# The order of a layer's small TensorE products: runs of full-height tiles, then of half-height tiles, partition halves alternating

## The chip, the cores and the metric

The kernel runs on one core of one Trainium2 chip. The metric is device time in microseconds (us), the median of several runs. A profile shows one further execution.

## What is computed

Two layers of a hybrid sequence model on 528 tokens (16 learned meta tokens ahead of 512) of width 1024. In each layer one wide projection feeds four mixers. Three of them work in chunks of tokens and matter here. The reference, cut down:

```python
def hybrid_layer(x, ...):
    h = rmsnorm(x, norm_mix) * mask
    (hg_q, hg_f, hg_i, hg_g, rt_q, rt_k, rt_v, rt_g, ss_u,
     gd_qkv, gd_b, gd_a, gd_g, gate) = _split(h @ w_in, IN_SPLITS)
    branches = (hgrn2_branch(...), retention_branch(...), s5_branch(...), gdn_branch(...))
    merged = sum over m of sigmoid(gates[m]) * (branches[m] @ w_branch[m])
    x = x + merged @ w_out
    h2 = rmsnorm(x, norm_ffn)
    gt, up = jnp.split(h2 @ w_gu, 2, axis=-1)
    return x + (jax.nn.silu(gt) * up) @ w_down

# gated linear attention and retention, chunk by chunk, 4 heads of 64 key and 128 value features
att = masked(q_t @ k_t.T)                # inside a chunk
o   = att @ v + q_t @ S                  # S: state handed over from the chunks before
S   = decay * S + k_end.T @ v
# gated delta rule: a unit triangular system per chunk and head
uw = triangular_solve(a0 + eye, rhs, lower=True, unit_diagonal=True)
```

## The kernel before

All weights are float32 and are split into a high and a low part of twelve bits; each panel of 128 columns is multiplied as high by high, high by low and low by high. These big products (`mmk`, line 206) are the main stream of TensorE: an operand tile of 128 by 128 against 264 or 256 tokens at a time. The mixers' own products are small and in plain float32. They are written as Python generators (`ret_gen` for retention, `gla_gen` for gated linear attention, `gdn_gen` for the gated delta rule, `s5_*` for the state space branch). A main-stream product calls `pump` before every fourth step of its contraction, and `pump` lets each running generator go on to its next `yield`. So TensorE's instruction order is exactly the order in which the program is written; a scheduler orders the other engines. What a generator emits between two yields is called a section below. A chunk has 128 tokens; there are four, and a short first one of 16.

A small product uses only the part of the 128 by 128 array that its operand covers. A profile row writes that as rows*columns. A state of one head has 64 rows, and two heads share the 128 partitions: head pair `p` = 0 lies on partitions 0 to 63 and `p` = 1 on 64 to 127.

- Outputs of a chunk in retention (lines 537 and 540) and in gated linear attention (lines 746 and 749): for each of the four heads, first `att @ v` with a 128*128 operand, then `q @ S` with a 64*128 operand added onto it. In the text the first kind is F (full height), the second H (half height). The order is F H F H F H F H.
- Blocks inside a chunk in gated linear attention: for `p` = 0 the products of blocks of 64 tokens (line 713, 64*64), then those between blocks of 16 (`cross`, line 695, 64*16); then the same for `p` = 1. Two later calls of `cross` do blocks of 32 and 64 in the same way.
- The triangular inverse in the gated delta rule, blocks of 32*32: two sections for a first product (line 1103, row blocks 0 and 2, 16 products each), then two for the next (lines 1112 and 1113 for row blocks 1 and 0, then 1113 for 2). `next(run)` (the first chunk's own work, lines 1040 and 1059 first) stands at the end of the second and the fourth section.

Every result goes to a PSUM tile of the pool `px` (`psx`), which has four buffers, and is read from there by ScalarE or VectorE: `tn_a` squares (line 371) and scales (line 382) the heads, `copy_predicated` (line 718) masks the blocks. In the last layer the short chunk has no outputs (`mute`).

Of the kernel before, what the change touches and what calls it, by code (L numbers as in the profile page):

```python
# [64 lines left out]
class Kern:  # L65
    """The main stream (projections, merges, feed forward) is plain code; the mixers between the projections are
    generators, whose parts are laid between its products: `pump` lets each running one go on to its next yield."""
# [112 lines left out]
    def wload(self, src, kt):  # L180
        """src [128, kt * 128]; returns k -> (high part, low part)"""
# [35 lines left out]
    def mm2(self, ws, kt, xh, xl, segs):  # L217
        """two products, both without their last operands at first: those come while others are used"""
# [46 lines left out]
    def rowpow(self, dst, src, scale, n):  # L265
        """dst = (src * scale + EPS) ** -0.5, tokens on partitions"""
# [51 lines left out]
    def norm_h(self, g):  # L318
        """finish of a norm: the operands hh, hl of the products that follow"""
# [15 lines left out]
    def norm_finish(self, h, n=KD):  # L335
        """the next n parts of a half"""
# [6 lines left out]
    def tail_hooks(self, kt):  # L343
        """the norm's first half, while the second half of its last operands is computed"""
# [3 lines left out]
    def head(self, srcs, segs):  # L348
        """the first two products after a norm, with its second half between those of the first"""
# [4 lines left out]
    def silu2(self, dst, ps, segs):  # L354
        """dst = 2 silu(ps)"""
# [31 lines left out]
    def tn_b(self, dst, c0, n, on, order):  # L387
        """dst[:, :, c0:c0+n] gets the normalised heads with features on partitions"""
# [6 lines left out]
    def head_gates(self, l, ct, segs):  # L395
        """2 silu of the gate columns of the heads"""
# [6 lines left out]
    def head_finish(self, gen, o, gs, ng, segs):  # L403
        """normalised heads times weight and gates; parts in float32r"""
# [44 lines left out]
    def mute(self, l, ci):  # L449
        """whether a chunk has only keys and values: the last layer's outputs for the meta tokens have no use"""  # L450
# [29 lines left out]
    def vt(self, v, ci, t0, n, name):  # L480
        """where the tokens-on-partitions copy of a chunk of v goes: its own place, but for the short chunk"""
        return self.ch(name) if ci == 0 else v[:, :, t0:t0 + n]

    def ret_gen(self, l, qk, v):
# [6 lines left out]
        for ci, (t0, n) in enumerate(CH):  # L491
# [69 lines left out]
    def lb_prep(self):  # L561
        """log lb and log(1 - lb) of the second layer: lb is the second part of a softmax of two"""
# [9 lines left out]
    def softplus(self, t, z):  # L572
        """t = ln(1 + exp(-|z|))"""
# [5 lines left out]
    def logsig(self, dst, z, t):  # L579
        """dst = min(z, 0) - ln(1 + exp(-|z|))"""  # L580
# [20 lines left out]
    def gla_gen(self, l, st, A, B):  # L601
# [5 lines left out]
        # keys, the cumulated log decays of blocks of 16 tokens, and the factors from them  # L607
# [72 lines left out]
        for ci, (t0, n) in enumerate(CH):  # L680
# [9 lines left out]
            def cross(pa, m, col):  # L690
                """products of the first and the second halves of the blocks of 2m tokens"""
                for j in range(2):
                    for c in range(0, n, 2 * m):
                        q0 = c + m
                        nc.tensor.matmul(pa[c:c + m, j, col(q0):col(q0) + m], ke[hs, j, c:c + m],
                                         qs[hs, j, q0:q0 + m], start=True, stop=True, skip_group_check=True)
# [9 lines left out]
            # inside the blocks of 32 tokens: products of blocks of 64, those of two blocks of 16 then overwritten  # L706
            for p in range(0 if self.mute(l, ci) else 2):
                hs = slice(64 * p, 64 * p + 64)
                pa = self.psx([P, 2, 64])
                w = min(64, n)  # L710
                for j in range(2):
                    for c in range(0, n, w):
                        nc.tensor.matmul(pa[c:c + w, j, :w], ks[hs, j, c:c + w], qs[hs, j, c:c + w], start=True,
                                         stop=True)
                if ci > 0:
                    cross(pa, 16, lambda t: t % 64)
                for c in range(0, n, w):
                    nc.vector.copy_predicated(att[c:c + w, 2 * p:2 * p + 2, c:c + w],
                                              k_["gm"][c:c + w, :w].unsqueeze(1).to_broadcast([w, 2, w]), pa[c:c + w, :, :w])
# [3 lines left out]
            if ci > 0:  # L723
                for m, dd, wd in ((16, de[:, :, 4 * (ci - 1):4 * ci], 32), (32, d32v[:, :, 2 * (ci - 1):2 * ci], 64),
# [3 lines left out]
                    for p in range(2 if wd else 0):  # L728
                        hs = slice(64 * p, 64 * p + 64)
                        pa = self.psx([P, 2, 64])  # L730
                        cross(pa, wd, lambda t: 0)
# [1026 lines left out]
```

## Time and profile before

| | |
|---|---|
| device time, median of 3 runs | 2272.08 us (2271.84 to 2274.5) |
| profiled execution, first to last instruction | 2275.3 us |
| TensorE products busy (PE) | 2241.9 us, 99% |
| TensorE weight loads busy (PEld) | 2045.0 us, 90% |
| VectorE (DVE) | 1283.5 us, 56% |
| ScalarE (ACT) | 893.8 us, 39% |
| GpSimd (POOL) | 249.3 us, 11% |
| mean share of the DMA engines in use, by 40 slices | 0.2 to 0.7 |

The profiled execution's time is its span; nothing is shown around it. PE and PEld are two views of the same engine: each product is a weight load and a matmul, and a plain float32 product shows as two of each. A busy PE says only that some product was under way, not that the array streamed at full rate. The rows of the timeline give the start of a group of alike instructions, how long it was under way, and how many there were; the distance from one group's start to the next group's start is what the group took from the engine.

### The profile page before, as it was taken

Reading aid. Unit: us, or ns where it says so; the run is one execution under the profiler, and the core shown is the slowest. Engines: PE = TensorE matmul, PEld = TensorE weight load, DVE = VectorE, ACT = ScalarE, POOL = GpSimd, SP = SyncE. Lnnn points to the kernel's source line nnn. Section 1 sums busy time; section 2 is a strip of 40 time slices with the busy share of each in tenths; the row PEclk is TensorE's granted clock in tenths of the full one; section 3 lists DMA queues with packets and bytes.
Section 4 is the critical chain, followed back from the end, with each engine's and each line's share of the span. In section 5 each row is a group of like instructions: output and inputs, shape, how many; then the busy total and the mean of one; then the engine's idle time right before and its main releaser. Section 6 shows DMA issues by size and latency. Waiting matters only on the chain. (4 is left out here: it accounts for less than half of the span.)

```text
span 2275.3 us, 41058 instructions
## 1 busy us (share of the span) xinstructions
PE 2241.9 (99%) x16288; PEld 2045.0 (90%) x16288; DVE 1283.5 (56%) x2440; ACT 893.8 (39%) x1921; POOL 249.3 (11%) x303
## 2 busy tenths in 40 slices
PE   9999999999999999999999899999999999999998
PEld 8999989899999999999999888787888888888886
DVE  6883566777644677533367944644375445434344
ACT  5643543333333443322346534633333434323232
POOL 2420111240000103200013201000000001000000
PEclk9999999999999999999999999999999999999999
DMA  3332222257223324432232232222452333332332
GB/s 118 96 92 83 85 66 77 92 165 214 75 89 107 113 90 136 133 86 93 86 120 81 90 102 79 70 66 70 151 162 85 97 121 98 93 95 92 99 92 82
DMA packets 147516, 229.73 MB, mean 101 GB/s; under 512 B 33116, under 2 KB 49956, under 8 KB 146812
## 3 DMA queue, kind: packets, MB, share of 16 engines
q1 hardware_dynamic: 139740, 209.38, 30.3%
q0 software_dynamic: 3840, 11.31, 1.5%
q10 hardware_dynamic: 3744, 6.42, 0.8%
q8 instruction: 128, 2.10, 0.4%
q14 instruction: 64, 0.52, 0.1%
HBM read 207.40 MB, written 19.65 MB: 100 GB/s over the span
## 5 line engine op out<-in xcount | busy, mean ns | idle before, releaser
L190 ACT CAST wh<-wr 128x512 fp32r<-128x512 f32 (+1 forms) x680 | 416.6, 614 | 1047.8 <-PE pm L206 861.5
L206 PE MATMUL pm<-hh,wh 128*128 128x264 f32 (+1 forms) x3120 | 800.0, 315 | 5.6 <-DVE x L1538 2.6
L206 PE MATMUL pm<-hl,wh 128*128 128x264 f32 (+1 forms) x3120 | 787.1, 311 | 2.8 <-DVE hl L200 1.2
L206 PE MATMUL pm<-hh,wl 128*128 128x264 f32 (+1 forms) x3120 | 783.1, 310 | 0.2 <-DVE wl L192 0.2
L192 DVE TENSOR_TENSOR wl<-wr,wh 128x512 fp32r<-128x512 f32 (+1 forms) x664 | 466.5, 705 | 551.8 <-ACT wh L190 527.0
L206 PEld LDWEIGHTS pm<-hh,wh 128*128 128x128 f32 x3120 | 513.4, 189 | 43.4 <-DVE x L1538 3.0
L206 PEld LDWEIGHTS pm<-hl,wh 128*128 128x128 f32 x3120 | 512.6, 188 | 35.6 <-DVE hl L200 3.0
L206 PEld LDWEIGHTS pm<-hh,wl 128*128 128x128 f32 x3120 | 512.4, 189 | 31.4 <-DVE wl L192 0.5
L206 PE MATMUL pm<-ah,wh 128*128 128x264 f32 (+2 forms) x542 | 146.1, 318 | 0.8 <-DVE x L1528 0.8
L206 PE MATMUL pm<-al,wh 128*128 128x264 f32 (+2 forms) x542 | 145.7, 317 | 0.0
L206 PE MATMUL pm<-ah,wl 128*128 128x264 f32 (+2 forms) x542 | 145.5, 317 | 0.0
L269 POOL TENSOR_TENSOR rs<-rs,mhalf 88x3 f32<-88x3 f32 (+1 forms) x10 | 8.7, 865 | 1056.5 <-ACT rs L268 1056.5
L206 PE MATMUL pm<-bh,wh 128*128 128x264 f32 (+1 forms) x384 | 105.4, 329 | 0.8 <-DVE mg L438 0.5
L206 PE MATMUL pm<-bh,wl 128*128 128x264 f32 (+1 forms) x384 | 102.4, 321 | 0.0
L206 PE MATMUL pm<-bl,wh 128*128 128x264 f32 (+1 forms) x384 | 102.3, 321 | 0.0
L206 PEld LDWEIGHTS pm<-ah,wh 128*128 128x128 f32 x542 | 91.3, 188 | 8.7 <-DVE x L1528 1.0
L206 PEld LDWEIGHTS pm<-al,wh 128*128 128x128 f32 x542 | 91.2, 188 | 7.2
L206 PEld LDWEIGHTS pm<-ah,wl 128*128 128x128 f32 x542 | 91.2, 188 | 6.9
L792 DVE SCALAR_TENSOR_TENSOR acc<-cvr,pk,acc 128x528 f32<-128x528 f32 x72 | 79.5, 1107 | 9.1 <-ACT acc L789 8.2
L206 PEld LDWEIGHTS pm<-bh,wh 128*128 128x128 f32 x384 | 63.5, 188 | 8.1 <-DVE mg L438 1.3
L438 DVE SCALAR_TENSOR_TENSOR th<-th,pm 128x528 f32<-128x528 f32 (+1 forms) x48 | 33.3, 694 | 65.7 <-PE pm L206 58.6
L206 PEld LDWEIGHTS pm<-bh,wl 128*128 128x128 f32 x384 | 63.7, 188 | 5.5
(409 smaller groups left out, 2610.1 us busy)
## 6 DMA issues: line engine op xcount, KB each, us to landing
wr<-in_w_in SPq DMA_DIRECT2D x304, 256.0 KB, 2.7
wr<-in_w_gu SPq DMA_DIRECT2D x176, 256.0 KB, 2.6
wr<-in_w_br SPq DMA_DIRECT2D x64, 256.0 KB, 2.6
wr<-in_w_dn SPq DMA_DIRECT2D x64, 256.0 KB, 2.6
wr<-in_w_out SPq DMA_DIRECT2D x32, 256.0 KB, 2.6
wr<-in_w_dn SPq DMA_DIRECT2D x32, 192.0 KB, 2.3
s5mi<-s5m ACTq DMA_DIRECT2D x16, 256.0 KB, 3.8
mi<-s5mi SPq DMA_DIRECT2D x16, 256.0 KB, 3.6
```

Source lines behind the costliest of these rows:

```text
L190: i = nc.scalar.copy(hi[:, :n], raw[:, :n])
L192: j = eng.tensor_tensor(out=lo[:, :n], in0=raw[:, :n], in1=hi[:, :n].bitcast(F32), op=ALU.subtract)
L206: self.nc.tensor.matmul(ps[:m, i, :n], wt, x[k][:, t0:t0 + n], start=(k == 0 and i2 == 0), stop=(k == kt - 1 and i2 == 2))
L269: nc.gpsimd.tensor_tensor(out=dst, in0=dst, in1=self.mhalf[:dst.shape[0], :n], op=ALU.pow)
L438: nc.vector.scalar_tensor_tensor(out=self.sv(th, segs), in0=self.sv(th, segs), scalar=1.0, in1=br, op0=ALU.add, op1=ALU.mult)
L792: nc.vector.scalar_tensor_tensor(out=acc, in0=raw[:, w:w + T], scalar=conv[:, jt + w:jt + w + 1], in1=acc, op0=ALU.mult, op1=ALU.add)
```

## The change

A new helper, `head_out`, makes the outputs of a chunk for both retention and gated linear attention: all four F products, then the four H products with the two partition halves alternating. Since an output's columns now begin in one run and are added to in another, only the first product into a PSUM tile has the start flag. In gated linear attention the two halves' block products are laid together, line 713's eight (alternating), then line 695's sixteen (alternating). In the gated delta rule the two sections of line 1103 become one with the two row blocks alternating, and those of lines 1112 and 1113 become one with three PSUM tiles; `next(run)` stands alone in a section behind each. The number of yields is the same. Comments and docstrings, which the change also removes, are left out here.

```diff
+    def head_out(self, att, vt, q, S, n):
+        mm = self.nc.tensor.matmul
+        pos = [self.psx() for _ in range(2)]
+        for p, po in enumerate(pos):
+            for j in range(2):
+                mm(po[:n, j, :], att[:n, 2 * p + j, :n], vt[:n, 2 * j + p, :], start=(j == 0),
+                   stop=(S is None and j == 1), skip_group_check=True)
+        if S is not None:
+            for j in range(2):
+                for p, po in enumerate(pos):
+                    hs = slice(64 * p, 64 * p + 64)
+                    mm(po[:n, j, :], q[hs, j, :n], S[hs, j, :], start=False, stop=(j == 1), skip_group_check=True)
+        return [(po, (p, 2 + p)) for p, po in enumerate(pos)]
...
-            parts = []
-            for p in range(0 if self.mute(l, ci) else 2):
-                po = self.psx()
-                for j in range(2):
-                    nc.tensor.matmul(po[:n, j, :], att[:n, 2 * p + j, :n], vt[:n, 2 * j + p, :], start=True,
-                                     stop=(ci == 0))
-                    if ci > 0:
-                        nc.tensor.matmul(po[:n, j, :], qz[64 * p:64 * p + 64, j, :n], R[64 * p:64 * p + 64, j, :],
-                                         start=False, stop=True)
-                parts.append((po, (p, 2 + p)))
+            parts = [] if self.mute(l, ci) else self.head_out(att, vt, qz, R if ci > 0 else None, n)
...
-            for p in range(0 if self.mute(l, ci) else 2):
-                hs = slice(64 * p, 64 * p + 64)
-                pa = self.psx([P, 2, 64])
+            if not self.mute(l, ci):
+                pas = [self.psx([P, 2, 64]) for _ in range(2)]
                 w = min(64, n)
                 for j in range(2):
                     for c in range(0, n, w):
-                        nc.tensor.matmul(pa[c:c + w, j, :w], ks[hs, j, c:c + w], qs[hs, j, c:c + w], start=True,
-                                         stop=True)
+                        for p, pa in enumerate(pas):
+                            hs = slice(64 * p, 64 * p + 64)
+                            nc.tensor.matmul(pa[c:c + w, j, :w], ks[hs, j, c:c + w], qs[hs, j, c:c + w], start=True,
+                                             stop=True)
                 if ci > 0:
-                    cross(pa, 16, lambda t: t % 64)
+                    cross(pas, 16, lambda t: t % 64)
...
-        for i in (0, 2):
-            pw = self.psx([P, 16, 32])
-            for x in range(16):
+        pws = [self.psx([P, 16, 32]) for _ in range(2)]
+        for x in range(16):
+            for i, pw in zip((0, 2), pws):
                 nc.tensor.matmul(pw[r[i + 1], x, :], gt[r[i], x, r[i + 1]], xn[r[i], x, 0:32], start=True, stop=True)
+        for i, pw in zip((0, 2), pws):
             nc.scalar.copy(w[r[i + 1], :, 0:32], pw[r[i + 1]])
-            if i == 2:
-                next(run)
-            yield
-        for i in (0, 2):
-            pz = self.psx([P, 16, 32])
-            for x in range(16):
-                if i == 0:
-                    nc.tensor.matmul(pz[r[1], x, :], xt[r[1], x, r[1]], w[r[1], x, 0:32], start=True, stop=True)
+        yield
+        next(run)
+        yield
+        pzs = [self.psx([P, 16, 32]) for _ in range(3)]
+        for x in range(16):
+            nc.tensor.matmul(pzs[2][r[1], x, :], xt[r[1], x, r[1]], w[r[1], x, 0:32], start=True, stop=True)
+            for i, pz in zip((0, 2), pzs):
                 nc.tensor.matmul(pz[r[i], x, :], w[r[i + 1], x, 0:32], xt[r[i + 1], x, r[i + 1]], start=True, stop=True)
```

How the order on TensorE moves is shown at two places. The first is the outputs of retention's first full chunk in the first layer; `att` and `rv` are the F operands, `R` and `qz` the H operands, and the number behind `px` tells the two PSUM tiles apart. Before:

```order
L531 MATMUL px_3871<-rv_1890,kt_3823 64x128 x4
L537 MATMUL px_3876<-rv_1890,att_3811 128x128
L540 MATMUL px_3876<-R_3724,qz_3773 128x128
L537 MATMUL px_3876<-rv_1890,att_3811 128x128
L540 MATMUL px_3876<-R_3724,qz_3773 128x128
L537 MATMUL px_3881<-rv_1890,att_3811 128x128
L540 MATMUL px_3881<-R_3724,qz_3773 128x128
L537 MATMUL px_3881<-rv_1890,att_3811 128x128
L540 MATMUL px_3881<-R_3724,qz_3773 128x128
```

The same place in the changed kernel, where line 463 has become the F products and line 469 the H products:

```order
L547 MATMUL px_3872<-rv_1890,kt_3824 64x128 x4
L463 MATMUL px_3877<-rv_1890,att_3812 128x128 x2
L463 MATMUL px_3878<-rv_1890,att_3812 128x128 x2
L469 MATMUL px_3877<-R_3725,qz_3774 128x128
L469 MATMUL px_3878<-R_3725,qz_3774 128x128
L469 MATMUL px_3877<-R_3725,qz_3774 128x128
L469 MATMUL px_3878<-R_3725,qz_3774 128x128
```

The same eight products stand in two runs instead of eight, and the second run alternates between the two tiles.

The second place, on TensorE too, is the first layer's triangular inverse, where `xn` and `gt` are the operands of line 1103, `vt` and `xt` those of the first chunk's own work, and line 206 the main stream. Before:

```order
L206 MATMUL pm<-hh,wl 128x264 x2
L1103 MATMUL px<-xn,gt 32x32 x16
L206 MATMUL pm<-hh,wh 128x264 x2
...
L1103 MATMUL px<-xn,gt 32x32 x16
L1059 MATMUL px<-vt,xt_2127 16x128 x4
L1040 MATMUL px<-k_ident,dv 128x128 x4
```

In the changed kernel (line 1103 has become 1106, 1059 has become 1062, and 1040 has become 1043):

```order
L206 MATMUL pm<-hh,wl 128x264 x2
L1106 MATMUL px<-xn,gt 32x32 x32
L206 MATMUL pm<-hh,wh 128x264 x2
...
L1062 MATMUL px<-vt,xt_2127 16x128 x4
L1043 MATMUL px<-k_ident,dv 128x128 x4
```

Two runs of sixteen have become one of thirty-two, and the first chunk's products stand by themselves.

## Rows read from the trace of the kernel before

**Rows 1.** The page, busy time of each engine (share of span, instructions).

```profile
PE 2241.9 (99%) x16288; PEld 2045.0 (90%) x16288; DVE 1283.5 (56%) x2440; ACT 893.8 (39%) x1921; POOL 249.3 (11%) x303
```

**Rows 2.** TensorE's waits: total us, times, longest.

```profile
PE px L964 <- DVE gam L966: 8.3, 2, 5.0
...
PE px L695 <- DVE ga L703: 1.9, 1, 1.9
```

**Rows 3.** Timeline of weight loads, retention's outputs: start, us under way, group.

```profile
306.65 0.30 PEld L537 LDWEIGHTS px<-rv,att 128*128 128x128 f32 x2 [0.17 <-DVE wl L192]
307.07 0.29 PEld L540 LDWEIGHTS px<-R,qz 64*128 64x128 f32 x2
...
309.57 0.29 PEld L540 LDWEIGHTS px<-R,qz 64*128 64x128 f32 x2
309.99 0.30 PEld L206 LDWEIGHTS pm<-bh,wh 128*128 128x128 f32 x2
```

**Rows 4.** Groups on TensorE by line and form: the H products.

```profile
L749 PE MATMUL px<-S,gb 64*128 64x128 f32 x64 | 15.5, 322 | 0.0
L540 PE MATMUL px<-R,qz 64*128 64x128 f32 x64 | 15.5, 322 | 0.0
```

**Rows 5.** Timeline of weight loads, a run of full-height float32 products.

```profile
196.39 0.98 PEld L1054 LDWEIGHTS px<-dS,dk 128*128 128x128 f32 x8
197.29 0.19 PEld L206 LDWEIGHTS pm<-hh,wh 128*128 128x128 f32 x1
```

**Rows 6.** Timeline of weight loads, retention's `att`: half-height products of both halves.

```profile
301.77 0.53 PEld L512 LDWEIGHTS px<-qk 64*128 64x128 f32 x8
302.42 0.20 PEld L519 LDWEIGHTS px<-k_ident,qz 128*128 128x128 f32 x2
```

**Rows 7.** Timeline of weight loads, block products of gated linear attention.

```profile
380.77 0.31 PEld L713 LDWEIGHTS px<-gb 64*64 64x64 f32 x8 [0.17 <-DVE s5t L1151]
381.15 0.18 PEld L695 LDWEIGHTS px<-gb,ga 64*16 64x16 f32 x16
381.36 0.31 PEld L713 LDWEIGHTS px<-gb 64*64 64x64 f32 x8
381.74 0.18 PEld L695 LDWEIGHTS px<-gb,ga 64*16 64x16 f32 x16
381.95 0.19 PEld L206 LDWEIGHTS pm<-hh,wh 128*128 128x128 f32 x1
```

**Rows 8.** Timeline of weight loads, the triangular inverse's four sections.

```profile
171.26 1.08 PEld L1103 LDWEIGHTS px<-xn,gt 32*32 32x32 f32 x32
172.38 0.30 PEld L206 LDWEIGHTS pm<-hh,wh 128*128 128x128 f32 x2
...
175.51 1.02 PEld L1103 LDWEIGHTS px<-xn,gt 32*32 32x32 f32 x30
176.42 0.11 PEld L1059 LDWEIGHTS px<-vt,xt 16*16 16x16 f32 x2
...
180.92 0.10 PEld L1112 LDWEIGHTS px<-xw,xt 32*32 32x32 f32 x1
180.93 0.10 PEld L1113 LDWEIGHTS px<-xt,xw 32*32 32x32 f32 x1
...
182.05 0.30 PEld L206 LDWEIGHTS pm<-hh,wh 128*128 128x128 f32 x2
...
185.18 1.08 PEld L1113 LDWEIGHTS px<-xt,xw 32*32 32x32 f32 x32
186.30 0.96 PEld L1070 LDWEIGHTS px<-vn,kt 16*128 16x128 f32 x8
```

**Rows 9.** Windows: busy us of each engine, granted clock, DMA share, GB/s.

```profile
430.00:440.00 10.00, 10.00 (x133) 9.44 (x133) 8.92 (x11) 4.14 (x10) 9.52 (x10) 1.00 0.25 81
440.00:450.00 10.00, 8.14 (x72) 7.90 (x71) 8.08 (x19) 2.54 (x6) 0.19 (x1) 1.00 0.27 80
1340.00:1344.00 4.00, 4.00 (x12) 2.72 (x10) 0.61 (x1) 0.19 (x1) 0.00 (x0) 0.57 0.23 70
```

More of the change, by code (lines that the diff above doesn't have):

```diff
@@ L688, in gla_gen, with cross @@
             ks, ke, qs = B[:, 2:4, t0:t0 + n], A[:, 2:4, t0:t0 + n], B[:, 0:2, t0:t0 + n]
-            def cross(pa, m, col):
+            def cross(pas, m, col):
                 for j in range(2):
@@ L694, in cross @@
                         q0 = c + m
-                        nc.tensor.matmul(pa[c:c + m, j, col(q0):col(q0) + m], ke[hs, j, c:c + m],
-                                         qs[hs, j, q0:q0 + m], start=True, stop=True, skip_group_check=True)
+                        for p, pa in enumerate(pas):
+                            hs = slice(64 * p, 64 * p + 64)
+                            nc.tensor.matmul(pa[c:c + m, j, col(q0):col(q0) + m], ke[hs, j, c:c + m],
+                                             qs[hs, j, q0:q0 + m], start=True, stop=True, skip_group_check=True)
             def widen(m, dd):
@@ L712, in gla_gen @@
                     for c in range(0, n, w):
-                        nc.tensor.matmul(pa[c:c + w, j, :w], ks[hs, j, c:c + w], qs[hs, j, c:c + w], start=True,
-                                         stop=True)
+                        for p, pa in enumerate(pas):
+                            hs = slice(64 * p, 64 * p + 64)
+                            nc.tensor.matmul(pa[c:c + w, j, :w], ks[hs, j, c:c + w], qs[hs, j, c:c + w], start=True,
+                                             stop=True)
                 if ci > 0:
-                    cross(pa, 16, lambda t: t % 64)
-                for c in range(0, n, w):
-                    nc.vector.copy_predicated(att[c:c + w, 2 * p:2 * p + 2, c:c + w],
-                                              k_["gm"][c:c + w, :w].unsqueeze(1).to_broadcast([w, 2, w]), pa[c:c + w, :, :w])
+                    cross(pas, 16, lambda t: t % 64)
+                for p, pa in enumerate(pas):
+                    for c in range(0, n, w):
+                        nc.vector.copy_predicated(att[c:c + w, 2 * p:2 * p + 2, c:c + w],
+                                                  k_["gm"][c:c + w, :w].unsqueeze(1).to_broadcast([w, 2, w]),
+                                                  pa[c:c + w, :, :w])
             yield
@@ L727, in gla_gen @@
                     yield
[L728 to L731, printed above, removed]
-                        for c in range(0, n, 2 * wd):
-                            nc.scalar.copy(att[c:c + wd, 2 * p:2 * p + 2, c + wd:c + 2 * wd], pa[c:c + wd, :, :wd])
+                    if wd:
+                        pas = [self.psx([P, 2, 64]) for _ in range(2)]
+                        cross(pas, wd, lambda t: 0)
+                        for p, pa in enumerate(pas):
+                            for c in range(0, n, 2 * wd):
+                                nc.scalar.copy(att[c:c + wd, 2 * p:2 * p + 2, c + wd:c + 2 * wd], pa[c:c + wd, :, :wd])
             if not last:
@@ L740, in gla_gen @@
             yield
-            parts = []
-            for p in range(0 if self.mute(l, ci) else 2):
-                po = self.psx()
-                hs = slice(64 * p, 64 * p + 64)
-                for j in range(2):
-                    nc.tensor.matmul(po[:n, j, :], att[:n, 2 * p + j, :n], vt[:n, 2 * j + p, :], start=True,
-                                     stop=(ci == 0))
-                    if ci > 0:
-                        nc.tensor.matmul(po[:n, j, :], qs[hs, j, :], S[hs, j, :], start=False, stop=True)
-                parts.append((po, (p, 2 + p)))
+            parts = [] if self.mute(l, ci) else self.head_out(att, vt, qs, S if ci > 0 else None, n)
             if parts:
@@ L1099, in gdn_gen @@
         r = [slice(32 * i, 32 * i + 32) for i in range(4)]
-        for i in (0, 2):
-            pw = self.psx([P, 16, 32])
-            for x in range(16):
+        pws = [self.psx([P, 16, 32]) for _ in range(2)]
+        for x in range(16):
+            for i, pw in zip((0, 2), pws):
                 nc.tensor.matmul(pw[r[i + 1], x, :], gt[r[i], x, r[i + 1]], xn[r[i], x, 0:32], start=True, stop=True)
+        for i, pw in zip((0, 2), pws):
             nc.scalar.copy(w[r[i + 1], :, 0:32], pw[r[i + 1]])
-            if i == 2:
-                next(run)
-            yield
-        for i in (0, 2):
-            pz = self.psx([P, 16, 32])
-            for x in range(16):
-                if i == 0:
-                    nc.tensor.matmul(pz[r[1], x, :], xt[r[1], x, r[1]], w[r[1], x, 0:32], start=True, stop=True)
+        yield
[5 more added lines that the diff above has]
+            for i, pz in zip((0, 2), pzs):
                 nc.tensor.matmul(pz[r[i], x, :], w[r[i + 1], x, 0:32], xt[r[i + 1], x, r[i + 1]], start=True, stop=True)
-            if i == 0:
-                nc.scalar.mul(xn[r[1], :, 0:32], pz[r[1]], -1.0)
+        nc.scalar.mul(xn[r[1], :, 0:32], pzs[2][r[1]], -1.0)
+        for i, pz in zip((0, 2), pzs):
             nc.vector.tensor_scalar(out=xt[r[i], :, r[i + 1]], in0=pz[r[i]], scalar1=-1.0, scalar2=None, op0=ALU.mult)
-            if i == 2:
-                next(run)
-            yield
+        yield
+        next(run)
+        yield
         lo, hi = slice(0, 64), slice(64, 128)
```

## The prediction

> **What bounds the kernel now.** I read the page's busy times first. TensorE's products are under way for 2241.9 of 2275.3 us, 99%, and VectorE, the next, for 56% [rows 1]. So nearly every microsecond on TensorE's path is a microsecond of the kernel, and what is not busy on TensorE is only 33.4 us in all. TensorE's own waits come next: the largest, 8.3 us in two waits, stands at the delta rule's products of queries and keys, which the change leaves alone; the only one in a line that it touches is 1.9 us, in `cross` [rows 2]. An order of products can therefore gain only if a busy TensorE wastes time, and the page cannot show that: a product that waits for the array to empty is counted as busy. The timeline can, by the distance from one group's start to the next.
>
> In the outputs of a chunk, F and H follow each other, and each product (two loads) takes 0.42 us from its start to the next kind's start; all eight take 309.99 - 306.65 = 3.34 us [rows 3]. Elsewhere, in a run of full-height float32 products without a change of tile shape, eight loads take 197.29 - 196.39 = 0.90 us, so 0.11 us for a load with its matmul and 0.22 for a product [rows 5]. Nearly half of each 0.42 is therefore the change of height: 0.20 us, in which the array empties and the first load of the new shape is exposed.
>
> What half-height products cost in a run is seen at retention's `att`, four products of the same size on both partition halves: 302.42 - 301.77 = 0.65 us for eight loads, the emptying behind them included [rows 6]. At 0.11 us a load behind each other, with the same exposed change, they would need 1.08. So the two halves of the array worked side by side.
>
> **The change, part by part.**
>
> *Outputs of a chunk.* Before: 3.34 us [rows 3]. After: the F run is the 0.42 of one product between two changes, and six further loads of 0.11: 1.08 us [rows 3, 5]. The H run is 0.65 us [rows 6]. Together 1.73, so 1.61 us less for a chunk. How often: lines 540 and 749 have 64 loads each, eight for a chunk, so 16 chunks in all [rows 4]. 16 x 1.61 = **25.8 us**. The trace has no H run that adds onto PSUM. The H products that now add cost the same 0.42 as the F products, which only write, so adding has no price of its own that shows [rows 3]. Bounds: if the halves did not work side by side, the run would take 1.08, and the term 16 x (3.34 - 2.16) = 18.9 us. I take the 25.8, since rows 6 have the same shape, type and size.
>
> *Blocks in gated linear attention.* Before: 0.38, 0.21, 0.38 and 0.21, from 380.77 to 381.95, 1.18 us [rows 7]. After: sixteen loads of line 713 on four tiles, then 32 of line 695 on eight. The first run should take the 0.38 of one half, because the second half runs on rows of the array that now idle. The second lies between 0.21 (all beside) and 0.42 (all behind); I take the middle, 0.32, because sixteen loads already start within 0.2 us and a limit on starting them may be near. So 1.18 - 0.70 = 0.48 us, for four chunks in two layers 8 x 0.48 = **3.8 us**, between 3.0 and 4.7. The later calls of `cross` had no change of shape between their halves; I put their gain at nothing.
>
> *Triangular inverse.* The first section took 172.38 - 171.26 = 1.12 us for 32 loads on one tile; the third, two tiles alternating, 182.05 - 180.92 = 1.13 for 64 loads [rows 8]. A second tile is free. So the merged first section should take 1.13, and the second section's 176.42 - 175.51 = 0.91 goes. The first chunk's products behind it stay; a first load that now comes exposed is about 0.1 at most. The merged next section has three tiles and 96 loads: 1.13 if the third is free too, and the 186.30 - 185.18 = 1.12 of the fourth goes. Both together, in two layers, 2 x (0.91 + 1.12) = **4.1 us**. Lower bound: if 64 loads in 1.13 were already the limit of starting them, 96 would take 1.70, and the term is 2 x (0.81 + 0.55) = 2.7. I take 4.1, as sixteen loads of line 695 get through in 0.21 [rows 7], five times as fast as one tile of line 1103.
>
> *What is hidden.* The moved `next(run)` keeps its distance in yields to all that reads its results. ScalarE's copies and VectorE's negations for the inverse now come in twos and threes behind one section; main-stream steps stand between them and their readers, and that cover of some 3 us is still there. In the outputs, ScalarE's squares of the first PSUM tile could start in the middle of the section and now start at its end, but the section ends 1.61 us sooner, so all are done sooner. Without that cover TensorE would wait for a `px` buffer (last rival).
>
> *What comes back.* Faster sections arrive earlier at what VectorE makes. In the first layer's gated linear attention VectorE is busy for 17.0 of 20 us, POOL alongside for 9.5 of the first 10, and TensorE is idle for 1.9 of the last 10 [rows 9], the one wait in `cross` [rows 2]. There VectorE's chain sets the time, and what a section just ahead saves (0.48, or 2.1 with the outputs) turns into more wait. Four chunks pass in this stage, but only one shows a wait; the price lies between nothing and 4 us, and I take 1.5, the larger part of that one chunk's saving.
>
> *The clock.* From 1340 to 1344 TensorE's granted clock is 0.57 on average, so mostly at 1.2 of 2.4 GHz, right behind the second layer's inverse with its small tiles [rows 9]. (1 - 0.57) x 4 = 1.7 us are lost there. A shorter row of small products may spare that, or a dip may come elsewhere. I take nothing, with 1.7 either way.
>
> **Sum.** 25.8 + 3.8 + 4.1 - 1.5 = 32.2 us. The profiled execution's 2275.3 becomes 2243.1. It is 3.2 us above the median of 2272.08, so I forecast 2272.1 - 32.2, rounded, **2240 us**.
>
> **Rivals.**
>
> 1. *The halves don't work side by side in the new runs*, for example because products that add onto PSUM keep the order. Then the outputs give 18.9 instead of 25.8, and the sum is 25.3: 2247 us. Rows 6 speak against it, though they write and don't add.
>
> 2. *Starting products is the limit.* If different tiles started no faster than one tile does in line 1103, 1.12 / 32 = 0.035 us a load [rows 8], then line 713's and 695's 48 loads would take 1.68 instead of 1.18 (8 x 0.5 = 4.0 lost), and the inverse's 64 and 96 would take 2.24 and 3.36 instead of 2.03 and 2.25 (2 x 1.3 = 2.6 lost). The sum is 25.8 - 4.0 - 2.6 - 1.5 = 17.7: 2254 us. Against it: 64 loads in 1.13 on two tiles [rows 8], sixteen in 0.21 [rows 7].
> The Trainium skill, "TensorE: Matmul & The Clock Gate", section "Wait — 56ns, not 53.3ns?", has such a rule: matmuls never start less than about 25 ns apart, however small. By that figure, as an estimate, the blocks would gain nothing and the inverse 0.6, and the kernel would take 2247; but line 695's sixteen loads in 0.21 us are 13 ns apart, and there the trace does not agree.
>
> 3. *Time is given back.* Were VectorE or ScalarE nearly late throughout the mixers' stages, half of 33.7 could return as waits: 2255 us. Only one wait of 1.9 in a touched line speaks for it [rows 2], and rows 9 show the fullest stage.
>
> 4. *Slower: PSUM buffers.* A grouped section holds two buffers of `px`, or three of four in the inverse, until its last product, and all readers start together. If TensorE then waited for a buffer in the next section, each of the 16 + 8 + 4 = 28 sections would have to lose over 33.7 / 28 = 1.2 us for the kernel to be slower; at 1.5 it takes 2272 + 8 = 2280. Against it: the number of buffers taken in a section of the outputs is two before and after, and TensorE's waits name no reader of these tiles [rows 2].
>
> That the change does not do what it says is out: TensorE's order is the program's, and it shows the runs.
>
> **How the numbers follow.** Chances: the forecast (about 2236 to 2244) 0.73; halves not side by side 0.10; the start limit 0.03; time given back 0.06; more than the upper sum 0.03; no change 0.02; slower by buffers 0.03. 0.2% of the time, 4.5 us, is about what a measurement can tell from no change. So faster 0.95, same 0.02, slower 0.03. Lower end of the time: 25.8 + 4.7 + 4.1 + 1.7 = 36.3 saved, nothing given back: 2236. Upper end by the low bounds: 18.9 + 3.0 + 2.7 - 4 - 1.7 = 18.9 saved: 2253; all of these at once is unlikely. 2235 to 2251 takes in the forecast and the first rival, and leaves out the start limit, the larger give-back, the last two cases and the case of more.
>
> **What would show it.** The timeline of a chunk's outputs should have two groups, eight F loads over about 1.08 us and eight H loads over 0.65, and TensorE's total distance there should be 1.73 instead of 3.34. If the H run takes 1.08, the first rival holds. Lines 713 and 695 (with new numbers) should show one group each, 0.38 and 0.32 us. The inverse's merged sections should take 1.13 each, the one with three tiles too; 1.7 or more there is the start limit. TensorE's waits should name nothing new over 2 us. A wait of TensorE for VectorE or ScalarE behind each of the 28 sections, or a busy time of TensorE that falls by 32 us while the span falls by half, would make the prediction wrong.

## Result: 2243.22 us, 30 us less than before

The changed kernel takes 2243.22 us in the median of four runs (2242.83 to 2244.98); the kernel before, run beside it, 2273.29 (2271.84 to 2275.21). The ratio is 0.9872, 95% interval 0.986 to 0.9883: 30.1 us less, where 32.2 were forecast. The profiled execution took 2244.98 us, its span 2243.2, 32.1 less than the span before.

The page of the changed kernel, busy times of the engines (answers to [rows 1]):

```profile
PE 2206.8 (98%) x16288; PEld 2022.1 (90%) x16288; DVE 1284.3 (57%) x2440; ACT 893.7 (40%) x1921; POOL 250.9 (11%) x303
```

TensorE's busy time fell by 35.1 us with the same 16288 products, and the other engines' times stayed. The span fell by 3.0 less than that: time in which TensorE waits has grown.

TensorE's waits after the change (answers to [rows 2]; line 704 was 695, 1106 was 1103):

```profile
PE px L704 <- DVE ga L712: 3.1, 1, 3.1
...
PE px L1106 <- DMA xn<-dg: 1.7, 2, 1.2
```

The wait in `cross` went from 1.9 to 3.1 us. A transfer, that of `xn` in the inverse, stands here for the first time.

The timeline of weight loads in the first full chunk of retention (answers to [rows 3]; line 463 is the F run, 469 the H run):

```profile
303.21 0.97 PEld L463 LDWEIGHTS px<-rv,att 128*128 128x128 f32 x8 [0.17 <-DVE wl L192]
304.30 0.52 PEld L469 LDWEIGHTS px<-R,qz 64*128 64x128 f32 x8
304.95 0.19 PEld L206 LDWEIGHTS pm<-bh,wh 128*128 128x128 f32 x1
```

Two groups stand where there were eight. F takes 304.30 - 303.21 = 1.09 us, H 0.65, both 1.74 instead of 3.34.

The blocks of gated linear attention (answers to [rows 7]; line 723 was 713):

```profile
370.92 0.32 PEld L723 LDWEIGHTS px<-gb 64*64 64x64 f32 x16 [0.17 <-DVE s5t L1154]
371.31 0.22 PEld L704 LDWEIGHTS px<-gb,ga 64*16 64x16 f32 x32
371.57 0.30 PEld L206 LDWEIGHTS pm<-hh,wh 128*128 128x128 f32 x2
```

0.39 and 0.26 us, 0.65 together instead of 1.18. The change also lays the halves of the two later calls of `cross` together; apart from the wait, nothing over 0.1 us came of that.

The inverse of the first layer, both merged sections, with the second one's first and last rows (answers to [rows 8]):

```profile
169.15 0.13 PEld L1106 LDWEIGHTS px<-xn,gt 32*32 32x32 f32 x2
169.94 1.08 PEld L1106 LDWEIGHTS px<-xn,gt 32*32 32x32 f32 x62 [0.65 <-DMA xn<-dg]
171.06 0.30 PEld L206 LDWEIGHTS pm<-hh,wh 128*128 128x128 f32 x2
...
178.65 0.10 PEld L1114 LDWEIGHTS px<-xw,xt 32*32 32x32 f32 x1
...
179.78 0.30 PEld L206 LDWEIGHTS pm<-hh,wh 128*128 128x128 f32 x2
```

and the first merged section of the last layer:

```profile
1307.84 0.13 PEld L1106 LDWEIGHTS px<-xn,gt 32*32 32x32 f32 x2 [0.36 <-issue]
1309.23 1.08 PEld L1106 LDWEIGHTS px<-xn,gt 32*32 32x32 f32 x62 [1.26 <-DMA xn<-dg]
1310.36 0.19 PEld L206 LDWEIGHTS pm<-hh,wh 128*128 128x128 f32 x1
```

The section with three tiles takes the forecast 1.13 us. The first one takes 1.91 and 2.52 us: it starts its first product and then stands still, since the second row block of `xn` has not landed. Without the hole its 64 loads need 1.13 too. Right behind the section of the last layer, TensorE's granted clock was low (columns as in [rows 9]):

```profile
1310.00:1314.00 4.00, 4.00 (x35) 3.18 (x29) 1.29 (x2) 2.31 (x4) 0.00 (x0) 0.57 0.44 143
```

Two windows behind the wait in `cross`:

```profile
430.00:435.00 5.00, 4.39 (x25) 4.30 (x26) 2.95 (x12) 0.42 (x2) 0.00 (x0) 0.50 0.32 90
435.00:440.00 5.00, 5.00 (x37) 5.00 (x37) 1.93 (x3) 1.16 (x3) 0.00 (x0) 0.83 0.14 49
```

Right behind the wait TensorE's granted clock is 0.50 for five microseconds, the lower of its two levels, and 0.83 on average in the next five. In the kernel before it stayed at 1.00 behind the wait there [rows 9].

### The profile page after: what moved, and what is told of

Same layout as the page of the kernel before. It is cut to its first block, busy times and chain, and to the rows that moved or that the text cites. A ratio compares the mean times of both kernels' runs of the same rounds, so it can differ in the third digit from the quotient of the medians.

```text
span 2243.2 us, 41058 instructions
## 1 busy us (share of the span) xinstructions
PE 2206.8 (98%) x16288; PEld 2022.1 (90%) x16288; DVE 1284.3 (57%) x2440; ACT 893.7 (40%) x1921; POOL 250.9 (11%) x303
```

## Experiments

All kernels compute the same as the changed one. Times are medians; a kernel's ratio is to the kernel before, run on the same chip in the same set. The changed kernel itself ran once more, beside experiments 5 and 6:

**The changed kernel again.** 

> The changed kernel once more, beside the two others of this set: every theory expects 2243 us (2241 to 2245), TensorE's wait of 3.1 us at line 704 in the first layer and the wait for the transfer of xn at line 1106 again.

Measured: 2244.72 us, ratio 0.987 (0.9855 to 0.9885). The wait in `cross` is 3.1 us again; that for `xn` is 2.7 in place of 1.7:

```profile
PE px L1106 <- DMA xn<-dg: 2.7, 2, 2.3
```

So the one wait repeats to a tenth, and the other moved by a microsecond between these two executions.

**1. Runs without alternation.**

```diff
         if S is not None:
-            for j in range(2):
-                for p, po in enumerate(pos):
+            for p, po in enumerate(pos):
+                for j in range(2):
```

and likewise at lines 704, 723, 1106 and 1116, so that each run has first one part of the array, then the next.

> The changed kernel with the same runs, but without alternation: in every run all products of one partition half (or row block) come first, then all of the other. Theory: it is the length of the runs that pays, and TensorE lets a few products of the second half pass those of the first, as it did in retention's `att` before. Then the H run of a chunk's outputs stays at 0.65 us and the block products near 0.39 and 0.26. The inverse's long runs (16 products on one tile, then 16 on the next) are too long to be passed: about 2.1 us for each merged section instead of 1.13 (the first of them without its wait for DMA), so the kernel is 0 to 4 us slower than the changed one. Rival: alternation is needed. Then each H run takes 1.08 (16 x 0.43 = 6.9 us), the blocks about 0.60 and 0.32 (8 x 0.27 = 2.2), and the inverse 2 to 4: 11 to 13 us slower than the changed kernel.

Measured: 2250.47 us, ratio 0.9901 (0.9876 to 0.9927). The timeline in this kernel, H run and then the inverse's three runs of 32:

```profile
307.53 0.53 PEld L469 LDWEIGHTS px<-R,qz 64*128 64x128 f32 x8
308.18 0.30 PEld L206 LDWEIGHTS pm<-bh,wh 128*128 128x128 f32 x2
...
178.53 1.02 PEld L1114 LDWEIGHTS px<-xw,xt 32*32 32x32 f32 x30
179.45 0.13 PEld L1117 LDWEIGHTS px<-xt,xw 32*32 32x32 f32 x2
...
179.53 1.91 PEld L1117 LDWEIGHTS px<-xt,xw 32*32 32x32 f32 x61
181.48 0.30 PEld L206 LDWEIGHTS pm<-hh,wh 128*128 128x128 f32 x2
```

H takes 0.65 us as before: four products of one half, then four of the other, work side by side without alternation. The blocks' sections did not change either, to within 0.1 us. In the inverse a run of 32 loads on one tile is hardly overtaken, and the section takes 2.95 us instead of 1.13. I had expected 2.1 there, from two runs where there are three. The ratio is 0.003 above that of the changed kernel, some 6.6 us, though the two intervals overlap. That lies between the two ranges expected, 0 to 4 and 11 to 13; the rows decide for the theory. These sections account for 2 x 1.8 = 3.6 of it; where the rest comes from is not shown.

**2. Four runs in a chunk's outputs instead of two.** F, H, F, H with two products each kind and tile:

```diff
         for p, po in enumerate(pos):
+            hs = slice(64 * p, 64 * p + 64)
             for j in range(2):
                 mm(po[:n, j, :], att[:n, 2 * p + j, :n], vt[:n, 2 * j + p, :], start=(j == 0),
...
-        if S is not None:
             for j in range(2):
-                for p, po in enumerate(pos):
-                    hs = slice(64 * p, 64 * p + 64)
+                if S is not None:
                     mm(po[:n, j, :], q[hs, j, :n], S[hs, j, :], start=False, stop=(j == 1), skip_group_check=True)
```

> The changed kernel, but a chunk's outputs in the order F F H H F F H H: four runs instead of two. Theory: a change of height costs 0.20 us, and H products of one half alone go one behind another at 0.11 us a load. Then each run takes 0.42 + 2 x 0.11 = 0.64, all four 2.56 instead of 1.73, and the kernel is 16 x 0.83 = 13 us slower than the changed one, about 2256. Rival: what cost time before was each return to the same PSUM columns (an H product added onto the F product just ahead of it), not the change of height. Then four runs, which put another product between the two, already give nearly all of it: about 2244.

Measured: 2256.14 us, ratio 0.9925 (0.9905 to 0.9945). Its timeline, the same chunk:

```profile
301.71 0.52 PEld L464 LDWEIGHTS px<-rv,att 128*128 128x128 f32 x4 [0.17 <-DVE wl L192]
302.35 0.52 PEld L468 LDWEIGHTS px<-R,qz 64*128 64x128 f32 x4
...
303.63 0.52 PEld L468 LDWEIGHTS px<-R,qz 64*128 64x128 f32 x4
304.27 0.30 PEld L206 LDWEIGHTS pm<-bh,wh 128*128 128x128 f32 x2
```

304.27 - 301.71 = 2.56 us. Two F products take 0.64, which is 0.42 for the one with the change and 0.22 for the two loads of the other, and two H products on one half take as much. The price of a chunk follows the number of changes of shape; the theory foretold both the section and the time. The rival falls: another product stood between the two on the same columns, and the cost was still there.

**3. The outputs alone**: the kernel before with `head_out` and nothing else of the change.

> The kernel before with the new order of a chunk's outputs alone. Theory: 16 x (3.34 - 1.73) = 25.8 us less than before, less 1 to 2 us given back in the first layer's gated linear attention: about 2248. Rival: the blocks and the inverse carry a third or more of the gain: 2253 or more.

Measured: 2249.28 us, ratio 0.9899 (0.9878 to 0.992), so 22 to 23 us of the kernel's 30, with chunks of 1.73 us. The wait in `cross` is here already 2.7 us, and TensorE's clock fell behind it:

```profile
435.00:440.00 5.00, 5.00 (x31) 5.00 (x31) 2.08 (x7) 0.89 (x2) 0.00 (x0) 0.69 0.37 105
```

16 x 1.6 = 25.6 us, less 0.8 of wait and some 1.5 in products at the lower clock, is about what the median shows.

**4. The inverse's merged first section one yield later**, behind the first chunk's own work:

```diff
+        next(run)
+        yield
         pws = [self.psx([P, 16, 32]) for _ in range(2)]
...
             nc.scalar.copy(w[r[i + 1], :, 0:32], pw[r[i + 1]])
-        yield
-        next(run)
         yield
```

> The changed kernel with the first chunk's own work ahead of the merged first section of the inverse instead of behind it, so that this section comes one pump later. Theory: the merged section waits for the DMA that brings the second of its two row blocks, which the kernel before needed only one pump later; the wait (0.75 and 1.37 us gaps in it) goes, both sections take 1.13, and the kernel is 2 us faster than the changed one. Rival: the DMA's time moves with the section, or the next section then waits for ScalarE's copies, which now have one pump instead of two: no gain.

Measured: 2242.9 us, ratio 0.9865 (0.9845 to 0.9886). In its timeline the section runs without a hole in both layers; the last layer's:

```profile
1314.09 1.09 PEld L1108 LDWEIGHTS px<-xn,gt 32*32 32x32 f32 x64 [0.36 <-issue]
1315.22 0.19 PEld L206 LDWEIGHTS pm<-hh,wh 128*128 128x128 f32 x1
```

1.13 us, and no wait for `xn` is left, so that wait was all that made the section longer. Behind the section TensorE's granted clock is now 1.00 in the last layer, where it was 0.57. But in the first layer the next section now took 1.72 us instead of 1.13, since ScalarE's copies came late (the rival's case, in one layer). The medians do not tell the two kernels apart.

**5. Retention's state products behind the outputs**, on top of experiment 4:

```diff
+            parts = [] if self.mute(l, ci) else self.head_out(att, vt, qz, R if ci > 0 else None, n)
             if not last:
                 pd = self.psx()
...
-            parts = [] if self.mute(l, ci) else self.head_out(att, vt, qz, R if ci > 0 else None, n)
```

> The changed kernel with the inverse's merged first section one yield later (as in the experiment before) and, in retention, the four state products (line 547, 128*64) behind a chunk's outputs instead of ahead of them. Theory: each change of tile shape costs 0.20 us whatever the products are. Ahead of the outputs the order has four changes (transposes or main stream to state products, to F, to H, to main stream); behind them it has three, since F then follows products of its own shape. Eight chunks have it, so 1.2 to 1.6 us beside the 2.2 us that the missing wait for the transfer gave in the trace: 2240 to 2241.5 us, F run 1.08 us with no other shape ahead, state products as long as before. Rival: the state is now ready 1.7 us later in every chunk, VectorE's update of it comes late, and the next chunk's H products or the main stream wait for it: new waits for VectorE at lines 469 or 528, and a time at or above the changed kernel's 2243.

Measured: 2240.58 us, ratio 0.9851 (0.9834 to 0.9867). The timeline of the second full chunk in the changed kernel, and below it in this one:

```profile
315.18 0.47 PEld L392 LDWEIGHTS px<-k_ident,on 128*128 128x128 f32 x4
315.81 0.42 PEld L547 LDWEIGHTS px<-rv,kt 128*64 128x64 f32 x8 [0.17 <-issue]
...
318.13 0.30 PEld L206 LDWEIGHTS pm<-hh,wh 128*128 128x128 f32 x2
```

and

```profile
315.87 0.47 PEld L392 LDWEIGHTS px<-k_ident,on 128*128 128x128 f32 x4
316.31 0.97 PEld L463 LDWEIGHTS px<-rv,att 128*128 128x128 f32 x8
...
318.63 0.30 PEld L206 LDWEIGHTS pm<-hh,wh 128*128 128x128 f32 x2 [0.17 <-issue]
```

2.95 and 2.76 us: the transposes of line 392 take 0.44 instead of 0.63, because F follows them in the same shape. One change less is 0.19 us. It shows in five chunks, not in eight: the last full chunk of a layer has no state products, and in the first full chunk of the first layer the transposes ahead have 16 rows, another shape. So the rows give 1.0 us where 1.2 to 1.6 were expected. No wait at line 469 or 528 came of it, so the rival falls. Experiments 4 and 5 together stand 4.1 us below the changed kernel of the same set; the intervals of the two ratios overlap a little.

**6. The tables' products on VectorE.** The state space branch makes its tables partly on GpSimd, in the stage of the wait in `cross`:

```diff
         def tp(out, x, y, op):
-            nc.gpsimd.tensor_tensor(out=out, in0=x, in1=y, op=op)
+            nc.vector.tensor_tensor(out=out, in0=x, in1=y, op=op)
```

> The changed kernel with the state space tables' products (line 1297, 128x512, 1.29 us each on GpSimd) on VectorE, where alike ones take 0.65 us. Theory of the contention: the wait of 3.1 us at line 704 stands behind VectorE work that is stretched while GpSimd works (line 441 3.23 us instead of 0.70, line 192 1.83 instead of 0.69, three of line 712 1.1 instead of 0.2, together about 6 us); without GpSimd's work line 441 takes 0.70 us there, and since VectorE gets six products of 0.65 = 3.9 us more in that stretch, the wait falls by about 2 us to 1 or less. Rival: the stretching was not GpSimd's doing, or VectorE simply has too much to do in that stage; then line 441 stays long, or the wait is 3 to 7 us, and the time is 2243 to 2247. In either case the rest of VectorE's added work, 11 us in each layer, lies where VectorE has room.

Measured: 2237.07 us, ratio 0.9835 (0.9821 to 0.985), 7.6 us below the changed kernel of its set. VectorE's timeline ahead of the wait in the changed kernel:

```profile
423.15 1.83 DVE L192 TENSOR_TENSOR wl<-wr,wh 128x512 fp32r<-128x512 f32 x1
424.90 3.23 DVE L441 TENSOR_TENSOR mg<-mg,th 128x528 f32<-128x528 f32 x1
```

GpSimd beside it:

```profile
423.12 1.30 POOL L1297 TENSOR_TENSOR s5e<-s5u 128x512 f32<-128x512 f32 x1
...
425.40 2.15 POOL L1297 TENSOR_TENSOR s5u<-s5pw,s5m 128x512 f32<-128x512 f32 x2
```

The same instructions on VectorE in this experiment:

```profile
423.44 0.68 DVE L1297 TENSOR_TENSOR s5e<-s5u 128x512 f32<-128x512 f32 x1
424.05 0.70 DVE L441 TENSOR_TENSOR mg<-mg,th 128x528 f32<-128x528 f32 x1
424.67 0.68 DVE L192 TENSOR_TENSOR wl<-wr,wh 128x512 fp32r<-128x512 f32 x1
```

Its page, busy times of the engines:

```profile
PE 2205.8 (99%) x16288; PEld 2021.8 (90%) x16288; DVE 1275.9 (57%) x2496; ACT 893.7 (40%) x1921; POOL 191.9 (9%) x247
```

Line 441 takes 0.70 us instead of 3.23, and line 192 0.68 instead of 1.83. The wait at line 704 is gone altogether, and with it the stretch of half clock: from 430 to 435 us the granted clock is 1.00. The products there take 5.9 us less (rows under *What comes back* below), which is most of the 7.6. VectorE has 56 instructions more and is busy for 8.4 us less than in the changed kernel.

The two stretched rows end 0.56 and 0.58 us behind the GpSimd products beside them (424.98 behind 424.42, 428.13 behind 427.55), a little less than such an instruction takes alone. GpSimd also issues a transfer there, but that is not the cause: in this experiment such an issue (424.43, 0.71 us) lies beside lines 441 and 192 and stretches neither. The Trainium skill, "SBUF — State Buffer", section "SBUF: two separate sides", has a rule that fits: a VectorE instruction with two inputs in SBUF and a GpSimd instruction that reads SBUF hold a pair of ports exclusively, and the later one waits. The lengths agree with it, 3.23 us against 0.70. The order of line 441 does not: its row begins 0.5 us ahead of GpSimd's two products, which by that rule would have had to wait. GpSimd's spans are rough, and no row here settles that. Line 438, one of whose two inputs lies in PSUM, took 0.69 us in the changed kernel at 308.80, beside a GpSimd product of line 521 (308.77, 0.73 us).

**7. The tables on VectorE in the kernel before**: the same edit without the change.

> The kernel before with the tables' products on VectorE alone. It tells how much of the 7.6 us belongs to the change. Theory: in the kernel before the wait was 1.9 us and TensorE's clock did not fall behind it; in the changed kernel it was 3.1 us with the clock at half for 6.8 us behind it, 6.5 us in the trace. So here only about 2 us are gained, 2270 to 2272 beside 2273, and the change itself gave back 6.5 - 1.9 = 4.6 us at this place. Rival: the stretched VectorE work cost the kernel before as much, in places that no wait names; then 5 to 8 us are gained, 2265 to 2268, and the change gave back little.

Measured: 2270.58 us, ratio 0.9987 (0.9978 to 0.9996), 3.2 us less than the kernel before. TensorE's waits name `cross` no more. So the wait of 1.9 was GpSimd's doing there too, but it was all that it cost: the same edit is worth 7.6 us behind the change and 3.2 ahead of it. The difference of 4.4 is what the change gave back at this place, by medians, which place it no better than by some 3 us. The expectation's 6.5 and 4.6 count too much for the clock: by the rows the edit saves 5.9 us there behind the change and 2.0 ahead of it, so 3.9 were given back.

**8. Everything that helped**: experiments 5 and 6 together.

> All that helped so far: the changed kernel, the inverse's merged first section one yield later, the state products behind the outputs, and the tables' products on VectorE. If the three gains are separate, 4.1 us (the first two, by the medians of the set before) and 7.6 (the third) add up: 2244.7 - 11.7, 2233 us, 2231 to 2235, with no wait at line 704 and none for the transfer of xn. Rival: the gains overlap, because all of them move when TensorE comes to the same stages; then 2235 to 2238, with a wait for VectorE that is new.

Measured: 2235.39 us, ratio 0.9832 (0.9818 to 0.9845), not to be told from experiment 6. A new wait took the place of an old one, in the first layer's inverse. From this kernel, TensorE's timeline, then ScalarE's:

```profile
179.74 0.10 PEld L1114 LDWEIGHTS px<-xw,xt 32*32 32x32 f32 x1 [1.91 <-ACT xw L1110]
```

```profile
178.47 0.62 ACT L190 CAST wh<-wr 128x512 fp32r<-128x512 f32 x1 [3.19 <-DMA wr<-in_w_in]
179.11 1.18 ACT L1110 COPY xw<-px 32x512 f32<-32x512 f32 x2
```

The copies that the next section reads stand behind a weight cast on ScalarE, and the cast waits 3.19 us for its transfer. One yield more between the section and its readers, which the changed kernel has, had hidden that.

**9. The later section in the last layer alone**, the rest as in 8. The edit of the inverse, against the changed kernel:

```diff
+        if l > 0:
+            next(run)
+            yield
         pws = [self.psx([P, 16, 32]) for _ in range(2)]
...
         yield
-        next(run)
-        yield
+        if l == 0:
+            next(run)
+            yield
```

> As the kernel with all changes, but the inverse's merged first section is one yield later in the last layer alone; in the first layer it stands as in the changed kernel. Theory: in the kernel with all changes the first layer lost about 4.4 us against the kernel with the tables alone, since the later section left its readers too little time: ScalarE's copies (line 1110) stood in line behind a weight cast (line 190) that waited for its transfer, and TensorE waited 1.9 and 0.5 us at line 1114, with its clock down behind it. In the last layer the same step gained 4.4 us, because there the wait for xn's transfer went. With each layer in its better form, 1.137 us for the second section in the first layer and 1.13 for the first section in the last, about 4 us less: 2231 to 2233 us. Rival: the copies are late in some executions whatever the place; then a wait at line 1114 stands in the first layer here too (the line's new number is 1120 or near), and the time is 2235 to 2237.

Measured: 2237.21 us, ratio 0.9841 (0.9828 to 0.9855). In its trace the wait at `xw` is gone, and the last layer's two merged sections take 1.13 and 1.14 us, as the theory says, yet the first layer's first section waits 1.2 us for `xn`.

The time did not follow: 2231 to 2233 were expected. It lies where the rival put it, but the rival's wait for ScalarE's copies is not in the trace. What these placements gain is less than what transfers and the clock move between executions (single runs of 6, 8 and 9 lie between 2233.3 and 2240.2). So experiments 6, 8 and 9 are the best versions, at 2235 to 2237, and which of them is best stays open.

## Why the prediction was right

The forecast of 2240 us missed by 3.2. Of this, 1.2 are the kernel before, whose median was 2272.08 at the forecast and is 2273.29 with a fourth run; the gain itself missed by 2.1. The main term, the outputs, held in size and mechanism. Two smaller ones did not: each made the gain more than 2 us too large, and that the miss came out smaller than their sum is partly luck.

*Outputs of a chunk*, forecast 25.8: 16 x (3.34 - 1.74) = 25.6 us. The halves work side by side when they add onto PSUM, so the first rival falls; experiment 3 measures this part alone, and experiment 2 shows that it is the number of changes that is paid.

*Blocks*, forecast 3.8: 8 x (1.18 - 0.65) = 4.2 us. Line 704's 32 loads took 0.26 us where the middle of 0.21 and 0.42 was taken. So starting products is no limit here, and the second rival falls.

*Inverse*, forecast 4.1: this is the step that failed. Before, the four sections took 1.12 + 0.91 + 1.13 + 1.12 = 4.28 us [rows 8]; now it is 1.91 + 1.13 in the first layer and 2.52 + 1.13 in the last (its second section took 1.14), so 1.9 us are saved in both by these rows, not 4.1. The term was sized as if the merged sections had nothing to wait for. It asked whether the products of the second row block have a tile that is free, and the paragraph on what is hidden only whether the results have time. Neither asked whether the operands are there: the section that was merged forward had stood 175.51 - 171.26 = 4.25 us later, and that had covered the transfer of `xn`. Experiment 4 shows that this is all of it.

The prediction had named 1.7 us or more in a merged section as the sign of a limit on starting products. 1.91 and 2.52 meet that sign, but the rows show a wait in the section, and 96 loads in 1.13 us speak against the limit. Its other sign, a new wait of TensorE over 2 us, did appear, in the repeat (2.3 us for `xn`). And line 695's loads, 0.21 / 16 = 0.013 us apart, start 2.7 times as fast as one tile of line 1103 with its 0.035, not five times; no term uses that factor.

*What comes back*, forecast 1.5: the right wait at the right place, and its growth of 1.2 us as expected. What was left out is the clock behind it. The stretch from the last main-stream step ahead of the wait to the first behind the next transposes holds the same products in all kernels. It is shown here for the kernel before, the changed one and experiment 6:

```profile
441.48 0.31 PEld L206 LDWEIGHTS pm<-hh,wl 128*128 128x128 f32 x2
447.44 0.30 PEld L206 LDWEIGHTS pm<-hh,wh 128*128 128x128 f32 x2
```

```profile
426.95 0.31 PEld L206 LDWEIGHTS pm<-hh,wl 128*128 128x128 f32 x2
430.58 0.54 PEld L704 LDWEIGHTS px<-gb,ga 64*64 64x64 f32 x8 [3.32 <-issue]
...
436.80 0.30 PEld L206 LDWEIGHTS pm<-hh,wh 128*128 128x128 f32 x2
```

```profile
426.96 0.31 PEld L206 LDWEIGHTS pm<-hh,wl 128*128 128x128 f32 x2
430.92 0.30 PEld L206 LDWEIGHTS pm<-hh,wh 128*128 128x128 f32 x2
```

It takes 5.96, 9.85 and 3.96 us, and 3.97 in experiment 7. So the change gave back 9.85 - 5.96 = 3.9 us here, 1.2 of them more wait and 2.6 to 2.7 products at the lower clock. The medians of experiments 6 and 7 give 4.4. Counting the clock by its share, (1 - 0.50) x 5 + (1 - 0.83) x 5 = 3.4, is too much: part of that time TensorE still waited, and two main-stream loads take 0.44 us at the lower level and 0.24 at the full one, which is less than twice as long.

*The clock*, forecast at nothing with 1.7 either way: nothing came of it, but by two moves that cancel, which is luck. Twelve main-stream loads of the last layer, from the first one's start to the last one's, take 2.43 us at the full clock. In the kernel before, those in the low stretch at 1340 [rows 9] took 3.70; that stretch is missing in the changed kernel, and in experiments 3 and 7 too, where the inverse has the old order. In the changed kernel, those behind the hole in the last layer's inverse took 3.97. This second stretch belongs to the step that failed: experiment 4 has neither the hole nor the low clock there.

Together 25.6 + 4.2 + 1.9 - 3.9 = 27.8 us. The medians give 30.1, with 26.6 to 31.8 by the interval of the ratio, so these runs show no gain beyond the sum. The spans give 32.1. Of that, 2.1 us stand ahead of anything that was changed: the first section of the inverse starts at 171.26 before [rows 8] and at 169.15 after, and the order up to there is the same. From 118 to 132 us TensorE's granted clock was 0.76 in the kernel before and 1.00 in the changed one; it was 0.76 in experiment 4, with the new order, and 1.00 in experiment 7, with the old one, so this belongs to the execution. The same holds for a wait of 0.98 us for ScalarE (line 789) at 1244.97 in the kernel before, which the changed kernel's trace lacks: experiment 1 has it, experiment 7 has not.

The third rival, half given back, and the fourth, waits for `px` buffers, fall: no wait stands behind the sections of the outputs, and TensorE's waits name no reader of their tiles.

## What to carry to other kernels

Where small products of different height stand among each other, count the changes of tile shape: here each cost 0.2 us in a TensorE that the page calls busy, and putting alike products in runs was worth more than any wait on the list. When work is merged forward, ask for each operand what had covered its arrival, not only where the results go. A wait is worth more than its length when TensorE's clock falls behind it: here 3.1 us of wait cost 5.9. That price is read from the distances of the same products at either clock; the share of the clock alone overstates it.

## What was not expected of the hardware

- Products of the other half of the array work beside a run of four on the first half without alternation (0.65 us in either order), but a run of 32 on one tile holds the next tile back (2.95 us for three runs, 1.13 alternating).
- VectorE's multiplication of two operands in SBUF took 3.23 us beside GpSimd's work and 0.70 without it, and moving GpSimd's products to the busier VectorE made the kernel 7.6 us faster.
- Behind waits of TensorE of 2.7 and 3.1 us in `cross` the clock fell to half; behind those of 1.9 and 2.2 us at the same place, in the kernel before and in experiment 2, it stayed at full. But in the changed kernel it also fell behind the wait of 1.26 us in the last layer's inverse, and in experiment 9 it stayed at full behind one of the same length in the first layer's. So these runs do not show what decides it.
